# Hybrid decoder layer on one core: row sums for four more block and pair combinations, made by one task, and all pairs of two more FFN blocks in seven products

## The chip, the core and the metric

The kernel runs on one core of a Trainium2 chip. The metric is the device time of one execution in microseconds (us). The kernel before took 1103.51 us in the median of three runs (1102.64 to 1104.92). TensorE (PE in the profile) multiplies into PSUM banks, VectorE (DVE) and ScalarE (ACT) work element by element, GpSimd (POOL) does small steps and issues some transfers, SyncE (SP) issues most of the others. Each engine takes its own instructions in the order in which they were written for it.

## What is computed

One layer over 256 tokens of width 2048: an RMS norm and one input projection; gated linear attention (GLA) over four heads; native sparse attention (NSA) over eight heads, with compressed, selected and window branches; an output projection with a residual; and a SwiGLU feed-forward part (FFN) of width 5632. Cut to what the change touches:

```python
def compress(u, pos, w1, w2):                   # u: keys or values of two heads
    blocks = u[:, :, cmp_idx] + pos             # 15 overlapping blocks of 32 positions
    flat = blocks.reshape(b_, hk, n_cmp, CMP_BLOCK * dh)
    return jax.nn.silu(flat @ w1) @ w2
...
h = x + jnp.concatenate([gla_out, nsa_out], axis=-1) @ w_out
m = rms_norm(h, ffn_norm_g)
return h + (jax.nn.silu(m @ w_gate) * (m @ w_up)) @ w_down
```

## The kernel before

**Two parts for every number.** A float32 factor is split into a high and a low part of the type that TensorE takes at full rate. A product is then three matmuls: high by high, high by low, low by high. For a weight, ACT copies the high part and DVE subtracts it from the raw tile to get the low part: `hi` and `lo` at L144 and L145 before the FFN, `ftwo` at L654 and L655 in it. There are four `lo` buffers of two row tiles each, so DVE can be at most four ahead of PE.

**Stages.** Until about 290 us eleven projections with W_in are made (`proj`, its matmuls at L292 in `chunk`), from 290 to 413 us W_out in two halves of eight chunks (`w_out_half`), after that eleven FFN blocks of 512 columns. In FFN block f, `gate_up(f)` (matmuls at L1164) makes the products with W_gate and W_up; `down(f-1)` then makes those with W_down for the block before (L292 again).

**Seven products.** In `gate_up` the 2048 rows of the weights are taken as eight pairs of row tiles. A pair with two halves of the tokens, and W_gate and W_up, is a product of 2x2 tiles. A plain pair takes eight tile products, 24 matmuls. A pair in the table `FIRST7` takes seven (the scheme of Strassen and Winograd), 21 matmuls; it needs sums of the tokens (`pair_forms`, made once) and sums of the weights. Before, blocks 2 to 9 take pair 6 plainly and the other seven pairs in seven products, and block 10 takes all eight in seven. Their orders are ORDER1 = (0,1,2,6,3,4,5,7) and ORDER = (0,...,7); the constant `ALL7` is the first block that has all eight.

**Row sums.** The sums of the weights are made in one of two ways. Either DVE makes them in the FFN when the pair is due: L1195 (1024 columns), L1196 and L1197 (512 each). Or they were made ahead: a task `sum_rows(f, pair)` loads the four row tiles of W_gate and W_up with two transfers of 512 KB on SP (L1091), adds them in place with four DVE instructions (L1096), and stores two results of 512 KB to DRAM from POOL (L1100); in the FFN they are fetched by POOL one pair ahead (L1153). Such a pair then loads three row tiles rather than four. The table `SUMS` lists 16 of them: (0,4), (1,2) to (1,5), pair 7 of blocks 2 to 10, and pairs 2 and 5 of block 10.

**What sets the order.** `drive` runs a main task (a projection, a half of W_out, a block) and gives it side tasks: GLA, NSA and the compression come up after so many units of matmul work (2 units each), and the first of the list `background`, the row sums, after every `rate[0]` units. A `sum_rows` task needs nine calls: three between the loads and the first addition, one for each addition, one after the stores, and one that ends it. A scheduler below puts each engine's instructions in order by its own estimate of when they can run; so the orders shift a little around any edit.

**Compression.** `positions` (L780) adds the positions to 16 of 32 rows of a block for both heads, as a tile of 16 x 2 x 15. `compress` runs in two passes (keys, values) of two halves. In each half 32 matmuls at L796 (16 in the program, two in the trace for each, since float32 passes in two) load 30 columns of weights into one of four column groups of 32; DVE clears the bank ahead, at L788, since columns 30 and 31 of a group are never written but are read with the rest. The rows of the compression's weights come by POOL transfers (L771).

Of the kernel before, what the change touches and what calls it, by code (L numbers as in the profile page):

```python
# [8 lines left out]
F32 = mybir.dt.float32  # L9
# [3 lines left out]
ALU = mybir.AluOpType  # L13
AX = mybir.AxisListType

P = 128
# [10 lines left out]
NCMP = 15  # L27
# [10 lines left out]
def kernel(  # L38
# [736 lines left out]
    def positions(w, half, new):  # L775

        blk, j0 = new([16, 2, NCMP]), 16 * half
        for h in range(2):
            u = st["uT"][:, w, h, j0:j0 + 240].rearrange("p (n j) -> p j n", j=16)
            TT(blk[:, :, h, :], u, pos[:, w, j0:j0 + 16].unsqueeze(2).to_broadcast([P, 16, NCMP]), ALU.add)  # L780
        return blk

    def compress():

        nxt = [st["rows"], w1_rows(1)]
        for w in range(2):
            ph = bank()
            nc.vector.memset(ph[:, :P], 0.0)  # L788
            for half in range(2):
# [4 lines left out]
                for j in range(16):  # L794
                    g = 32 * (j % 4)
                    mm(ph[g:g + N2, :P], blk[:, j].rearrange("p h n -> p (h n)"), r[j // 8][:, j % 8, :], start=(half == 0 and j < 4),  # L796
                       stop=(half == 1 and j >= 12), tile_position=(0, g), skip_group_check=True)
                    if j % 16 == 15:
                        yield
# [217 lines left out]
    ALL7 = 10  # L1017
# [67 lines left out]
    def sum_rows(f, pair):  # L1085

        n_tiles[0] += 1
        gate, up = g4([2, 512]), g4([2, 512])
        for to, m in ((gate, w_gate), (up, w_up)):
            with behind(last["dma"]):  # L1090
                nc.sync.dma_start(to, m[0][2 * pair * P:(2 * pair + 2) * P, f * FB:(f + 1) * FB].rearrange("(k p) w -> p k w", p=P))  # L1091
        for _ in range(3):
            yield True
        for o, i in ((up[:, 0], up[:, 1]), (up[:, 1], gate[:, 1]), (gate[:, 1], up[:, 0]), (gate[:, 0], gate[:, 1])):
            with behind(last["d"]):
                TT(o, o, i, ALU.add)  # L1096
            yield True
        to = row_sums[f, pair] = [dp.tile([P, 2, 512], F32, name=f"sums{i}_{f}_{pair}") for i in range(2)]
        for part, a in zip(to, (up, gate)):
            nc.gpsimd.dma_start(part, a)  # L1100
        for _ in range(1):
            yield True
# [265 lines left out]
    background += [sum_rows(f, pair) for f in sorted(SUMS) for pair in SUMS[f]]  # L1368
    rate[0] = 12
# [3 lines left out]
    rate[0] = 26  # L1373
# [3 lines left out]
    rate[0] = 18  # L1377
# [5 lines left out]
    rate[0] = 14  # L1383
# [43 lines left out]
```

## Time and profile before

| what | us |
|---|---|
| median of three runs | 1103.51 |
| lowest, highest | 1102.64, 1104.92 |
| the profiled execution | 1103.67 |
| its span, first to last instruction | 1102.0 |
| PE busy, DVE busy, ACT busy, POOL busy | 1094.4, 991.5, 742.0, 73.1 |
| W_out's second half ends, FFN begins | 413 |
| an FFN block's period (blocks 8 and 9) | 61.95, 61.94 |

The profiled execution took 1.67 us more than its span, which lies before the first and after the last instruction. A row of a timeline gives the start, the duration, the engine, the line of the kernel, the operation and the tiles (output, arrow, inputs); in brackets stands how long the engine sat idle before it and what ended that. "SPq" or "PEq" is an engine's sequencer, which issues and waits. A row of stretches gives for each engine its busy time and the number of its instructions, then the granted clock, the share of the transfer engines and GB/s. Matmuls overlap: a matmul of 512 columns shows some 390 ns, but the next one starts 0.23 us after it, so PE's work is counted by starts. The granted clock is 1.00 throughout.

### The profile page before, as it was taken

The page shows a single profiled execution, that of the slowest core. Times are in us where ns is not written, and L with a number is a line of the kernel's source. Part 1 is how long each engine was busy: PE and PEld are TensorE (multiplying, and loading weights), DVE is VectorE, ACT ScalarE, POOL GpSimd, SP SyncE. Part 2 cuts the span into 40 slices and gives each one's busy share as a digit, 9 for nine tenths or more (in the row PEclk, how much of TensorE's full clock was granted, in tenths as well). Part 3 has the DMA queues.
Part 4 walks back from the last instruction along what each step waited for, and adds up shares of the span by engine and source line. Part 5 has one row for each costly group of instructions (what it writes and reads, how often), then busy time and mean ns, then how long its engine had stood idle before and what let it go on. Part 6 is the DMA issues. An engine that isn't in the chain of part 4 may idle for free.

```text
span 1102.0 us, 14594 instructions
## 1 busy us (share of the span) xinstructions
PE 1094.4 (99%) x5290; PEld 900.6 (82%) x5290; DVE 991.5 (90%) x1277; ACT 742.0 (67%) x1009; POOL 73.1 (7%) x134
## 2 busy tenths in 40 slices
PE   9999999999999999999999999999999999999998
PEld 8888888987787877888888888888888888888886
DVE  6678879987799688997999999999999999999997
ACT  6645557555675587667586866768586866768685
POOL 4110001132100000000000000000000000000000
PEclk9999999999999999999999999999999999999999
DMA  7999988467864547785566657576566657576773
GB/s 269 340 340 368 354 295 292 160 226 285 287 229 173 191 153 244 234 318 188 182 230 210 214 200 251 175 257 210 202 230 210 215 199 251 174 259 231 234 230 114
DMA packets 124850, 259.61 MB, mean 236 GB/s; under 512 B 6709, under 2 KB 8793, under 8 KB 124778
## 3 DMA queue, kind: packets, MB, share of 16 engines
q1 hardware_dynamic: 113514, 219.86, 58.3%
q0 software_dynamic: 10368, 37.75, 9.3%
q10 hardware_dynamic: 896, 1.07, 0.3%
q8 instruction: 41, 0.67, 0.2%
q14 instruction: 31, 0.25, 0.1%
HBM read 239.78 MB, written 18.87 MB: 235 GB/s over the span
## 4 chain that ended last, share of the span: by engine, by line
PE 94%; DVE 3%; DMA 1%; POOL 1%; ACT 1%; issue 1%; ACTq 0%; SPq 0%; DVEq 0%; POOLq 0%
PE bank L292 47%; PE bank L1164 39%; PE bank L217 3%; PE bank L1305 2%; PE bank L889 1%; PE bank L962 1%; POOL sm L220 1%; DMA raw<-in_w_in_dram 1%; DMA g<-in_w_up_dram 1%; DVE lo L145 0%; PE bank L597 0%; DVE g L637 0%; PE bank L796 0%; DVE g L592 0%; DVE g L638 0%
## 5 line engine op out<-in xcount | busy, mean ns | idle before, releaser
L1164 PE MATMUL bank<-ftwo,g 128*128 128x512 f32 x1848 | 431.7, 392 | 0.2 <-ACT ftwo L654 0.2
L1164 PEld LDWEIGHTS bank<-ftwo,g 128*128 128x128 f32 x1848 | 342.5, 188 | 76.5 <-DVE ftwo L655 3.3
L292 PE MATMUL bank<-hi,g 128*128 128x512 f32 (+1 forms) x1088 | 325.2, 377 | 0.5 <-ACT hi L332 0.5
L655 DVE TENSOR_TENSOR ftwo<-fraw,ftwo 128x1536 fp32r<-128x1536 f32 (+1 forms) x130 | 257.6, 1982 | 8.2 <-ACT ftwo L654 6.8
L654 ACT ACTIVATE ftwo<-fraw 128x1536 fp32r<-128x1536 f32 (+1 forms) x130 | 217.0, 1671 | 32.0 <-DMA fraw<-in_w_up_dram 22.9
L292 PE MATMUL bank<-ftwo,g 128*128 128x512 f32 x960 | 221.1, 391 | 0.0
L292 PEld LDWEIGHTS bank<-hi,g 128*128 128x128 f32 x1088 | 192.0, 188 | 31.1 <-issue 1.4
L292 PEld LDWEIGHTS bank<-ftwo,g 128*128 128x128 f32 x960 | 179.2, 188 | 39.2 <-ACT bank L1276 1.9
L292 PE MATMUL bank<-lo,g 128*128 128x512 f32 (+3 forms) x544 | 193.9, 376 | 0.4 <-DVE lo L333 0.3
L144 ACT ACTIVATE hi<-raw 128x1024 fp32r<-128x1024 f32 (+3 forms) x124 | 130.5, 1057 | 86.0 <-PE bank L292 64.1
L145 DVE TENSOR_TENSOR lo<-raw,hi 128x1024 fp32r<-128x1024 f32 (+3 forms) x124 | 149.7, 1217 | 35.3 <-ACT hi L144 34.8
L654 ACT ACTIVATE ftwo<-g 128x1024 fp32r<-128x1024 f32 x74 | 78.2, 1057 | 69.9 <-DVE g L1195 40.6
L292 PEld LDWEIGHTS bank<-lo,g 128*128 128x128 f32 x544 | 98.5, 189 | 15.0 <-DVE lo L333 0.8
L655 DVE TENSOR_TENSOR ftwo<-g,ftwo 128x1024 fp32r<-128x1024 f32 x74 | 90.2, 1218 | 10.5 <-ACT ftwo L654 10.5
L655 DVE TENSOR_TENSOR ftwo<-fsum,ftwo 128x1024 fp32r<-128x1024 f32 x74 | 90.1, 1217 | 0.0
L654 ACT ACTIVATE ftwo<-fsum 128x1024 fp32r<-128x1024 f32 x74 | 77.5, 1048 | 6.9 <-DVE fsum L1197 5.7
L1288 ACT COPY g<-bank 128x512 f32<-128x512 f32 x80 | 45.9, 589 | 38.8 <-PE bank L292 37.1
L1195 DVE TENSOR_TENSOR g<-fraw 128x1024 f32<-128x1024 f32 x56 | 67.4, 1216 | 0.0
L1276 ACT COPY bank<-g 128x512 f32<-128x512 f32 x80 | 45.2, 593 | 14.4 <-DVE f L1225 13.2
L654 ACT ACTIVATE g<-bank 128x512 fp32r<-128x512 f32 x46 | 27.2, 598 | 32.1 <-PE bank L217 26.6
L217 PE MATMUL bank<-ident,g 128*128 128x128 f32 (+3 forms) x230 | 43.3, 276 | 0.2 <-DVE g L737 0.2
L1153 POOL DMA_DIRECT2D g<-sums x16 | 8.5, 533 | 510.8 <-DVE ftwo L655 482.2
(244 smaller groups left out, 899.8 us busy)
## 6 DMA issues: line engine op xcount, KB each, us to landing
fraw<-in_w_gate_dram SPq DMA_DIRECT2D x86, 512.0 KB, 4.0
fraw<-in_w_down_dram SPq DMA_DIRECT2D x42, 1024.0 KB, 5.1
raw<-in_w_in_dram SPq DMA_DIRECT2D x36, 1024.0 KB, 7.6
fraw<-in_w_up_dram SPq DMA_DIRECT2D x70, 512.0 KB, 4.8
sums<-g POOLq DMA_DIRECT2D x32, 512.0 KB, 6.4
raw<-in_w_out_dram SPq DMA_DIRECT2D x16, 1024.0 KB, 5.2
g<-in_w_gate_dram SPq DMA_DIRECT2D x16, 512.0 KB, 7.3
g<-in_w_up_dram SPq DMA_DIRECT2D x16, 512.0 KB, 8.9
```

Source lines behind the costliest of these rows:

```text
L144: act(h[:, i:i + n], r[:, k + i:k + i + n], AF.Copy)
L145: last["d"] = TT(o[:, i:i + n], r[:, k + i:k + i + n], f32(h[:, i:i + n]), ALU.subtract)
L217: return nc.tensor.transpose(o, i, ident[:n, :n])
L220: nc.gpsimd.tensor_tensor(o, i, mhalf[:i.shape[0], :i.shape[1]], ALU.pow)
L292: last["mm"] = mm(bk[t], a[:, k, t * P:(t + 1) * P], m[:, off:off + w], start=(first_ and k == 0 and i == 0), stop=(end and k == 3 and i = ...
L654: act(hi, ps, AF.Copy)
L655: last["d"] = TT(lo, ps, f32(hi), ALU.subtract)
L1164: mm(banks[q], x, m, start=todo[q] == total[q], stop=todo[q] == 1)
L1195: TT(s1, r[:, 1:3], r[:, 3:4].to_broadcast([P, 2, 512]), ALU.add)
L1276: nc.scalar.copy(banks[qs[n][t]], h_sb[n][:, t, :])
L1288: nc.scalar.copy(h_sb[n][:, t, :], bs[t])
L1305: mm(bk, u, m, start=(first and i == 0), stop=(end and i == 2), skip_group_check=onto)
```

## The change

**FFN.** `ALL7` goes from 10 to 8. Blocks 8 and 9 then take all eight pairs in seven products, in ORDER, and `SUMS` gains (8,2), (8,5), (9,2), (9,5): 20 combinations.

**Row sums as one task.** `rows_for` issues the two loads; `all_sums` goes through the list, asks for the next combination's rows before it adds the present one's, and stores without a call of its own. Each combination now takes five calls, and the rates are 22, 46 and 32 units where they were 12, 26 and 18; the last stays 14, and is no longer set a second time.

**Compression.** The tile of `positions` is 16 x 32; POOL clears its last two columns, the matmuls load 32 columns, and the bank isn't cleared by DVE.

```diff
     def positions(w, half, new):
-        blk, j0 = new([16, 2, NCMP]), 16 * half
+        full, j0 = new([16, 32]), 16 * half
+        nc.gpsimd.memset(full[:, :, N2:], 0.0)
+        blk = full[:, :, :N2].rearrange("p j (h n) -> p j h n", h=2)
...
-        return blk
+        return full
     def compress():
...
-            nc.vector.memset(ph[:, :P], 0.0)
...
-                    mm(ph[g:g + N2, :P], blk[:, j].rearrange("p h n -> p (h n)"), r[j // 8][:, j % 8, :], start=(half == 0 and j < 4),
+                    mm(ph[g:g + 32, :P], blk[:, j], r[j // 8][:, j % 8, :], start=(half == 0 and j < 4),
...
-    ALL7 = 10
+    ALL7 = 8
...
-    def sum_rows(f, pair):
-        n_tiles[0] += 1
-        gate, up = g4([2, 512]), g4([2, 512])
-        for to, m in ((gate, w_gate), (up, w_up)):
+    def rows_for(f, pair):
+        res = g4([2, 512]), g4([2, 512])
+        for to, m in zip(res, (w_gate, w_up)):
             with behind(last["dma"]):
                 nc.sync.dma_start(to, m[0][2 * pair * P:(2 * pair + 2) * P, f * FB:(f + 1) * FB].rearrange("(k p) w -> p k w", p=P))
+        return res
+
+    def all_sums(todo):
+        nxt = rows_for(*todo[0])
         for _ in range(3):
             yield True
-        for o, i in (...):
-            with behind(last["d"]):
-                TT(o, o, i, ALU.add)
+        for at, (f, pair) in enumerate(todo):
+            gate, up = nxt
+            if at + 1 < len(todo):
+                nxt = rows_for(*todo[at + 1])
             yield True
-        to = row_sums[f, pair] = [...]
-        for part, a in zip(to, (up, gate)):
-            nc.gpsimd.dma_start(part, a)
-        for _ in range(1):
-            yield True
+            for o, i in (...):
+                with behind(last["d"]):
+                    TT(o, o, i, ALU.add)
+                yield True
+            to = row_sums[f, pair] = [...]
+            for part, a in zip(to, (up, gate)):
+                nc.gpsimd.dma_start(part, a)
...
-    background += [sum_rows(f, pair) for f in sorted(SUMS) for pair in SUMS[f]]
-    rate[0] = 12
+    background.append(all_sums([(f, pair) for f in sorted(SUMS) for pair in SUMS[f]]))
+    rate[0] = 22
...
-    rate[0] = 26
+    rate[0] = 46
...
-    rate[0] = 18
+    rate[0] = 32
```

The additions stand at L1106 in the changed program (L1096 before), the stores at L1110 (L1100), the fetches at L1161 (L1153); other lines of the later part move by 1 (to L1001) or by 8.

Three places show how the order moves. The first is DVE in W_out's first half, at its fourth chunk, whose first low part is `lo_3378` before and `lo_3385` after; `g_578` or `g_528` are rows being added, `sm` is NSA's soft-max, L655 makes low parts for NSA. Before:

```order
L915 TENSOR_TENSOR g_569_3239<-sm_3227,sm_3234 128x4x3x15
L921 TENSOR_SCALAR g_546_3123<-g_546_3123,sm_3242 128x256 x4
L921 TENSOR_SCALAR g_547_3124<-g_547_3124,sm_3242 128x256 x4
L655 TENSOR_TENSOR g_584_3286<-bank_3284,g_583_3285 128x512
L895 TENSOR_REDUCE sm_3330<-bank_3334 128x2
L145 TENSOR_TENSOR lo_3378<-raw_3375,hi_3377 128x2x512
L655 TENSOR_TENSOR g_572_3254<-bank_3255,g_571_3253 128x4x128
L896 TENSOR_SCALAR sm_3331<-sm_3330,sc_3022 128x2
L1096 TENSOR_TENSOR g_578_3266<-g_578_3266 128x512
```

And after:

```order
L922 TENSOR_SCALAR g_535_3127<-g_535_3127,sm_3243 128x256 x4
L655 TENSOR_TENSOR g_569_3284<-bank_3282,g_568_3283 128x512
L1106 TENSOR_TENSOR g_528_3088<-g_528_3088 128x512
L896 TENSOR_REDUCE sm_3337<-bank_3341 128x2
L896 TENSOR_REDUCE sm_3337<-bank_3357 128x2
L655 TENSOR_TENSOR g_560_3255<-bank_3256,g_559_3254 128x4x128
L1106 TENSOR_TENSOR g_528_3088<-g_528_3088,g_527_3087 128x512
L897 TENSOR_SCALAR sm_3338<-sm_3337,sc_3018 128x2 x2
L1106 TENSOR_TENSOR g_527_3087<-g_527_3087,g_528_3088 128x512
L145 TENSOR_TENSOR lo_3385<-raw_3382,hi_3384 128x2x512
```

Three additions and three NSA steps now stand ahead of this low part; two more additions do so further up, between it and the low part before it.

The second place is PE at the same chunk: L292 is W_out, L889 to L892 (L890 to L893 after) are NSA's scores, L217 transposes. Before:

```order
L892 MATMUL bank_3333<-kcm,g_561_3192 128x15
L292 MATMUL bank_3291<-hi_3377,g_438_2608 128x512
L292 MATMUL bank_3291<-lo_3378,g_438_2608 128x512
L889 MATMUL bank_3391<-g_318_1976,g_562_3193 128x256
L292 MATMUL bank_3291<-hi_3377,g_439_2609 128x512
```

And after:

```order
L893 MATMUL bank_3340<-kcm,g_549_3192 128x15
L292 MATMUL bank_3289<-hi_3384,g_426_2601 128x512
L890 MATMUL bank_3398<-g_307_1970,g_550_3193 128x256
L890 MATMUL bank_3398<-g_308_1971,g_550_3193 128x256
L292 MATMUL bank_3290<-hi_3384,g_426_2601 128x512
L890 MATMUL bank_3398<-g_307_1970,g_551_3194 128x256
L892 LDWEIGHTS identb
L892 MATMUL bank_3398<-cneg,identb 128x256
L893 MATMUL bank_3340<-kcm,g_549_3192 128x15
L217 MATMUL bank_3440<-ident,g_557_3240 79x128 x4
L217 MATMUL bank_3451<-ident,g_534_3126 128x128 x2
L217 MATMUL bank_3451<-ident,g_535_3127 128x128 x2
```

The next row after is the first use of `lo_3385`: five score matmuls, one of W_out and eight transposes were put ahead of it.

The third place is POOL around the compression: L220 raises to the power -1/2, L771 asks for rows of the compression's weights. Before:

```order
L220 TENSOR_TENSOR sm_2451<-sm_2451,mhalf 128x2
L771 DMA g_429_2539<-in_cmp_k_w_dram 128x8x128
L220 TENSOR_TENSOR sm_2480<-sm_2480,mhalf 128x2
L771 DMA g_430_2541<-in_cmp_k_w_dram 128x8x128
L771 DMA g_435_2599<-in_cmp_v_w_dram 128x8x128
L220 TENSOR_TENSOR sm_2530<-sm_2530,mhalf 128x2
L771 DMA g_436_2601<-in_cmp_v_w_dram 128x8x128
L1100 DMA sums_8_7_2639<-g_361_2231 128x1024
```

And after:

```order
L220 TENSOR_TENSOR sm_2475<-sm_2475,mhalf 128x2
L771 DMA g_417_2533<-in_cmp_k_w_dram 128x8x128
L220 TENSOR_TENSOR sm_2524<-sm_2524,mhalf 128x2
L771 DMA g_418_2535<-in_cmp_k_w_dram 128x8x128
L771 DMA g_423_2591<-in_cmp_v_w_dram 128x8x128
L771 DMA g_424_2593<-in_cmp_v_w_dram 128x8x128
L778 MEMSET g_425_2595 128x16x2
L778 MEMSET g_476_2817 128x16x2
L778 MEMSET g_482_2875 128x16x2
```

The second transfer of the keys' rows moves behind a third L220, and the clearing of the position tiles stands behind four transfers.

More of the change, by code (lines that the diff above doesn't have):

```diff
@@ L1083 @@
     row_sums = {}
-    def sum_rows(f, pair):
-        n_tiles[0] += 1
-        gate, up = g4([2, 512]), g4([2, 512])
-        for to, m in ((gate, w_gate), (up, w_up)):
+    def rows_for(f, pair):
+        res = g4([2, 512]), g4([2, 512])
+        for to, m in zip(res, (w_gate, w_up)):
             with behind(last["dma"]):
                 nc.sync.dma_start(to, m[0][2 * pair * P:(2 * pair + 2) * P, f * FB:(f + 1) * FB].rearrange("(k p) w -> p k w", p=P))
+        return res
+    def all_sums(todo):
+        nxt = rows_for(*todo[0])
         for _ in range(3):
             yield True
-        for o, i in ((up[:, 0], up[:, 1]), (up[:, 1], gate[:, 1]), (gate[:, 1], up[:, 0]), (gate[:, 0], gate[:, 1])):
-            with behind(last["d"]):
-                TT(o, o, i, ALU.add)
+        for at, (f, pair) in enumerate(todo):
+            gate, up = nxt
+            if at + 1 < len(todo):
+                nxt = rows_for(*todo[at + 1])
             yield True
-        to = row_sums[f, pair] = [dp.tile([P, 2, 512], F32, name=f"sums{i}_{f}_{pair}") for i in range(2)]
-        for part, a in zip(to, (up, gate)):
-            nc.gpsimd.dma_start(part, a)
-        for _ in range(1):
-            yield True
+            for o, i in ((up[:, 0], up[:, 1]), (up[:, 1], gate[:, 1]), (gate[:, 1], up[:, 0]), (gate[:, 0], gate[:, 1])):
+                with behind(last["d"]):
+                    TT(o, o, i, ALU.add)
+                yield True
+            to = row_sums[f, pair] = [dp.tile([P, 2, 512], F32, name=f"sums{i}_{f}_{pair}") for i in range(2)]
+            for part, a in zip(to, (up, gate)):
+                nc.gpsimd.dma_start(part, a)
     rf = kp.tile([P, NT], F32, name="rf")
@@ L1382 @@
     drain(later)
-    rate[0] = 14
     drive([w_out_half(1)], 6)
```

## The prediction

> **What bounds the kernel now.** I read the page first, then the chain in order of time, then what PE waited for.
>
> ```profile
> span 1102.0 us, 14594 instructions
> PE 1094.4 (99%) x5290; PEld 900.6 (82%) x5290; DVE 991.5 (90%) x1277; ACT 742.0 (67%) x1009; POOL 73.1 (7%) x134
> ...
> PE 94%; DVE 3%; DMA 1%; POOL 1%; ACT 1%; issue 1%; ACTq 0%; SPq 0%; DVEq 0%; POOLq 0%
> ```
>
> PE is busy for 99% of the span and holds 94% of the chain that ended last. A busy PE may still be a stalled one, so the list of its waits matters: it has six rows, and its two longest are
>
> ```profile
> PE bank L207 <- DVE g L201: 1.3, 1, 1.3
> PE bank L796 <- DVE g L780: 1.1, 1, 1.1
> ...
> ```
>
> The first is the start of the program. The second is the only wait in the change's reach that an earlier operand would shorten: one half of the compression. So the kernel lasts as long as its matmuls: what saves matmuls saves their full time, and what merely relieves another engine saves nearly nothing. The chain through the last FFN blocks shows what one saved product is worth. In block 9 and then in block 10 it reads:
>
> ```profile
> 956.88 0.22 PE bank L217 x2
> ...
> 960.54 32.88 PE bank L1164 x144
> ...
> 1022.45 32.22 PE bank L1164 x141
> ```
>
> Block 9 still has a plain pair and block 10 none: 144 against 141 matmuls in the long piece, all else equal. 32.88 us over 144 is 0.228 us a matmul, and 32.88 - 32.22 = 0.66 us is what the plain pair costs more.
>
> **FFN blocks 8 and 9.** Each loses one plain pair's 24 matmuls and gains 21, so 6 matmuls go: 6 x 0.228 = 1.37 us. The Trainium skill, page TensorE: Matmul & The Clock Gate, section Back-to-back issue gap, gives 131 ns as the sustained spacing of matmuls of 512 columns and 216 ns as the isolated one; by these the six would be an estimated 0.79 or 1.30 us, and the spacing of this trace decides against both. The term stands only if no other engine becomes late. Here are `gate_up` of blocks 9 and 10, then the whole periods:
>
> ```profile
> 953.36:993.42 40.06, 40.06 (x180) 32.64 (x180) 39.10 (x37) 27.65 (x26) 2.12 (x4) 1.00 0.64 221
> 1015.30:1054.67 39.37, 39.37 (x177) 31.99 (x177) 38.88 (x36) 29.17 (x28) 2.11 (x4) 1.00 0.71 228
> 953.36:1015.30 61.94, 61.94 (x276) 50.58 (x276) 60.62 (x57) 44.22 (x47) 2.12 (x4) 1.00 0.67 230
> 1015.30:1076.50 61.20, 61.20 (x277) 49.83 (x277) 58.77 (x62) 47.70 (x53) 2.11 (x4) 1.00 0.68 219
> ```
>
> DVE (the third pair of numbers) works 60.62 of block 9's 61.94 us. That is the resource to count. The forms of its instructions:
>
> ```profile
> L655 DVE TENSOR_TENSOR ftwo<-fraw,ftwo 128x1536 fp32r<-128x1536 f32 x74 | 129.8, 1754 | 3.6 <-ACT ftwo L654 2.9
> L655 DVE TENSOR_TENSOR ftwo<-fraw,ftwo 128x2048 fp32r<-128x2048 f32 x56 | 127.8, 2283 | 4.7 <-ACT ftwo L654 3.9
> L655 DVE TENSOR_TENSOR ftwo<-g,ftwo 128x1024 fp32r<-128x1024 f32 x74 | 90.2, 1218 | 10.5 <-ACT ftwo L654 10.5
> L655 DVE TENSOR_TENSOR ftwo<-fsum,ftwo 128x1024 fp32r<-128x1024 f32 x74 | 90.1, 1217 | 0.0
> L1195 DVE TENSOR_TENSOR g<-fraw 128x1024 f32<-128x1024 f32 x56 | 67.4, 1216 | 0.0
> L1197 DVE TENSOR_TENSOR fsum<-fsum,fraw 128x512 f32<-128x512 f32 x56 | 38.4, 686 | 0.9
> L1196 DVE TENSOR_TENSOR fsum<-g,fraw 128x512 f32<-128x512 f32 x56 | 38.3, 686 | 0.7
> ...
> L1240 DVE TENSOR_TENSOR f<-bank,f 128x512 f32<-128x512 f32 x21 | 14.3, 679 | 0.1
> ```
>
> Pair 6 gives up one of 2283 ns and takes one of 1754 and two of 1218 and 1217: +1.91 us, and sums of 1216 + 686 + 686 = 2.59 us. Pairs 2 and 5 lose these sums, -5.18 us, since theirs now come from DRAM. The plain pair's eighth bank isn't added any more (L1240): -0.68 us. Together -1.36 us a block, so DVE would work 59.3 us of 61.3. ACT, 44.22 us busy, has 17.7 idle for its own exchange (one copy of 2048 columns for one of 1536 and two of 1024). POOL fetches four more results a block, as block 10 does. Block 10 is the test that before already holds: its `gate_up` takes 39.37 us with all of PE busy. I take the full 1.37 us; below 0 and above 1.5 are excluded by that row.
>
> **Additions asked for ahead.** DVE's waits for the rows of the sums are the edit's plain target:
>
> ```profile
> DVE g L1096 <- DMA g<-in_w_up_dram: 11.6, 5, 5.1
> ```
>
> 11.6 us in five waits can go. They are DVE's, though, and no wait of PE names the weights' low parts (L145) that stood behind them: the four buffers covered them. Gain taken: 0. Until the end of the fifth projection the four-step additions do not get denser: by the 57th low part DVE has made 39 of them before and 36 after, in the stretch where the transfers are full:
>
> ```profile
> 87.00:110.00 23.00, 23.00 (x107) 19.04 (x106) 20.03 (x30) 13.06 (x19) 2.13 (x4) 1.00 0.98 362
> ```
>
> Asking one combination ahead puts about 1 MB earlier into that stream, 3 us at 362 GB/s, ahead of some weights of W_in. The rows that it delays are asked for three chunks ahead, so I take 0 here too, and 1 us at worst.
>
> **Four more combinations.** The 16 further additions fall into W_out's two halves:
>
> ```profile
> 306.88:316.54 9.66, 9.66 (x55) 7.62 (x54) 9.05 (x29) 7.56 (x15) 0.00 (x0) 1.00 0.90 315
> 310.00:350.00 40.00, 40.00 (x212) 31.93 (x211) 37.38 (x101) 24.76 (x61) 1.67 (x3) 1.00 0.65 238
> 350.00:386.00 36.00, 36.00 (x173) 29.50 (x172) 25.80 (x35) 19.23 (x29) 1.78 (x3) 1.00 0.52 176
> ```
>
> From 350 us on DVE has 10 us to spare in 36, and the transfers are half idle, which covers three combinations of four additions and 2 MB each. From 310 to 350 DVE has 2.6 us left in 40, and the tightest point lies at its entry, the fourth chunk of W_out:
>
> ```profile
> 316.54 1.21 DVE L145 TENSOR_TENSOR lo<-raw,hi 128x1024 fp32r<-128x1024 f32 x1
> ...
> 326.77 0.68 DVE L1096 TENSOR_TENSOR g<-g 128x512 f32<-128x512 f32 x1
> 327.37 0.21 DVE L909 TENSOR_REDUCE sm<-sm 128x4 f32<-128x60 f32 x1
> ```
> ```profile
> 319.07 0.28 PE L889 MATMUL bank<-g,g 128*128 128x256 f32 x1
> 319.19 0.40 PE L292 MATMUL bank<-lo,g 128*128 128x512 f32 x1
> ...
> 320.36 0.39 PE L292 MATMUL bank<-lo,g 128*128 128x512 f32 x1
> ```
>
> The low part ends at 316.54 + 1.21 = 317.75, and PE first uses it at 320.36: 2.6 us of slack. In the new order five additions at 0.60 (326.77 to 327.37) and NSA steps of about 1.2 us (one L655, as long as an addition, and four short ones) stand ahead of it, 4.2 us, less the 0.6 us that DVE idles in 306.88 to 316.54: 3.6 us later, 1.0 us too late by itself. But PE's order moves with it: eight transposes (0.22 a pair, 0.88), a matmul (0.23) and five score matmuls (0.12 each from 319.07 to 319.19, 0.6) now come first, 1.7 us. So the low part should be in time by about 0.7 us. I take 0 for W_out, and 4.2 us as the other end, if nothing covers; a gain is excluded, as no wait of PE lies here.
>
> **Compression.** The wait of 1.1 us that PE has here comes from this order on DVE:
>
> ```profile
> 251.85 0.68 DVE L1096 TENSOR_TENSOR g<-g 128x512 f32<-128x512 f32 x1
> 252.45 1.01 DVE L780 TENSOR_TENSOR g<-g,cols 128x240 f32<-128x240 f32 x2
> 253.38 1.22 DVE L145 TENSOR_TENSOR lo<-raw,hi 128x1024 fp32r<-128x1024 f32 x1
> ```
> ```profile
> 253.52 1.08 PE L796 MATMUL bank<-g,g 128*30 128x128 f32 x32 [1.10 <-DVE g L780]
> ```
>
> In the changed order the addition stands behind L780, so the positions are ready 0.60 us earlier: -0.6 us. Against it stands POOL, where the second transfer of the keys' rows moves behind a third power step:
>
> ```profile
> 246.14 1.62 POOL L220 TENSOR_TENSOR sm<-sm,mhalf 128x2 f32<-128x2 f32 x1 [0.83 <-DVE sm L631]
> 247.72 0.92 POOL L771 DMA_DIRECT2D g<-in_cmp_v_w_dram  x1
> ```
> ```profile
> DMA to landing us min/median/max: 4.7/6.7/9.1
> ```
>
> The last row is for all eight transfers of these rows. Behind the power step this one is issued at 247.72 (where before asks for rows of the values) and lands 4.7 to 9.1 us later, at 252.4, 254.4 or 256.8. It holds the second half of the rows, which PE needed 0.5 us after 253.52, at 254.0. So the half ends 0.6 us earlier, 0.4 or 2.8 us later than before. I take the median, +0.4 us. The cleared tile is ready in time: four transfers of 0.92 us, less the first, and a short clear end at 250.7, and the bank's own clear was waited for by nobody.
>
> The matmuls load 32 columns for 30:
>
> ```profile
> L796 PEld LDWEIGHTS bank<-g,g x128: 104/108/108, 247.2 to 281.0; 128*30 128x30 f32 x128
> ```
>
> A load takes 108 ns, four at a time in four column groups. The Trainium skill, page TensorE: Matmul & The Clock Gate, section LDWEIGHTS (loading the stationary operand), has a load grow with its columns, P/1.2 ns; by that the change adds an estimated 1.7 ns a load, 0.2 us over 128. The row is four times what that formula gives for 30 columns (25 ns), so I go by the row. Four groups of matmuls of 1.08 us each, longer by 2 columns in 30, give 4 x 1.08 x 2/30 = 0.3 us if the loads set the pace and 0 if they don't; I take 0.1.
>
> **The sum.** -1.37 (FFN) + 0.4 (compression) + 0.1 (columns) = -0.87 us. From the profiled execution's 1103.67 that is 1102.8; its median stands 0.16 lower, at 1103.51, so the forecast is **1102.7 us**. About 0.2%, 2.2 us, is what a measurement of this kernel can tell from no change, since its three runs lie 2.3 us apart; the forecast is inside it.
>
> **Rivals.**
>
> *DVE falls behind in W_out (slower).* If NSA's steps can't run early enough for PE's new order, since the score matmuls and transposes put ahead wait for DVE themselves, nothing covers the additions at the fourth chunk, and PE waits the 4.2 us: 1103.67 - 1.37 + 0.5 + 4.2 = 1107.0. For it speaks DVE's 37.38 of 40 us; against it that no wait of PE lies here now and that the transposes read what the soft-max steps had finished by then. It turns the gain into a loss once PE waits more than 0.9 us there. 0.10.
>
> *The compression's rows land late.* The second transfer takes 9.1 us like the slowest: 1103.67 - 1.37 + 2.8 + 0.1 = 1105.2. Against it: that row is from all eight, and the slowest of them may lie where the transfers were full. 0.08.
>
> *They land early.* Then only the positions decide, and the wait shrinks by 0.6: 1103.67 - 1.37 - 0.6 = 1101.7. For it speaks 4.7 us, the fastest; the transfer needs 5.7 us or less. 0.30.
>
> *The sums aren't there.* A combination that isn't stored when its block is written would be summed on DVE: pairs 2 and 5 then cost 5.18 us again, and a block would need 60.62 - 1.36 + 5.18 = 64.4 us of DVE against 61.3 of PE, 3.1 us twice: 1103.67 + 2 x 3.1 - 0.87 + 1.37 = 1110.4. POOL's order has all twenty pairs of stores ahead of the first fetch, so 0.01.
>
> **How the numbers follow.** The forecast keeps 0.51. A median of three scatters by some 0.7 us here. Under 1101.3 (faster by over 0.2%) lie a third of the early case, 0.10, and 0.03 of the forecast's; over 1105.7 lie 0.08 of W_out's case and 0.02 of the late case. That is 0.13 faster, 0.10 slower and 0.77 the same. The range goes from 1101.0, the early case less the scatter, to 1105.0, just short of the late case; what it leaves out above is W_out's case and half of the late one.
>
> **What would show it.** In the changed profile, the long piece of L1164 in blocks 8 and 9 counts 141 matmuls and 32.2 us, and the periods are 61.3; if they are 61.9, DVE or a fetch is late and the FFN term falls. DVE's wait for rows of the sums is gone or below 2 us, with PE's time before the FFN the same. PE's row at the compression's second half shows a wait between 0.5 and 1.5 us, by a transfer rather than by L780. W_out shows no wait of PE over 0.5 us near 320 us. The forecast is wrong if the first FFN matmul of the long series comes more than 2 us earlier or later than now while the blocks behave.

## The result: 0.8% slower

The changed kernel took 1112.66 us in the median of five runs (1111.27 to 1113.06), the kernel before 1102.75 (1102.52 to 1104.92) beside it: a ratio of 1.0082, 95% interval 1.007 to 1.0093. The forecast was 1102.7 us, in a range of 1101.0 to 1105.0. The profiled execution of the changed kernel took 1111.27 us, its span is 1109.5.

The profile after, first the page:

```profile
span 1109.5 us, 14659 instructions
...
PE 1094.3 (99%) x5284; PEld 898.9 (81%) x5284; DVE 997.9 (90%) x1287; ACT 743.4 (67%) x1013; POOL 81.7 (7%) x154
...
PE 87%; DVE 5%; DMA 4%; issue 2%; ACT 1%; POOL 1%; SPq 0%; ACTq 0%; DVEq 0%; POOLq 0%
```

PE's busy time is the same to 0.1 us. Its share of the chain that ended last fell from 94 to 87%: DVE (3 to 5%) and DMA (1 to 4%) hold more of it. The FFN isn't where that comes from. The chain through blocks 8 and 9 (start, duration, what, how many):

```profile
900.32 3.54 PE bank L1172 x15
...
907.51 32.32 PE bank L1172 x141
...
961.62 3.54 PE bank L1172 x15
...
968.82 32.28 PE bank L1172 x141
```

141 matmuls in 32.3 us, and the period of block 8 is 961.62 - 900.32 = 61.30 us: as forecast. To find the loss I took three low parts (`lo`) and read on PE's timeline when the same one is first used. Before:

```profile
185.85 0.39 PE L292 MATMUL bank<-lo,g 128*128 128x512 f32 x1
...
255.45 0.48 PE L292 MATMUL bank<-lo,g 128*128 128x512 f32 x1
...
410.64 0.39 PE L292 MATMUL bank<-lo,g 128*128 128x512 f32 x1
```

And after:

```profile
185.51 0.39 PE L292 MATMUL bank<-lo,g 128*128 128x512 f32 x1
...
261.66 0.48 PE L292 MATMUL bank<-lo,g 128*128 128x512 f32 x1
...
418.94 0.39 PE L292 MATMUL bank<-lo,g 128*128 128x512 f32 x1
```

The lag, after less before, is -0.34, 6.21 and 8.30 us. So 6.55 us are lost between 186 and 255 us, in the stretch where GLA and NSA's keys run beside the projections, and 2.09 from there to the end of W_out; the granted clock is 1.00 in both. The first FFN blocks add 0.7 (block 2's first product comes 107.09 us after block 0's, 106.40 before), blocks 8 and 9 take 1.3 off, and the program up to 186 us gave 0.3; that is 7.7 us, close to the 7.5 by which the span grew. What the engines wait for, the rows that are new:

```profile
ACT g L748 <- DMA sums<-g: 6.3, 1, 6.3
POOL g L771 <- DMA sums<-g: 5.9, 1, 5.9
...
DVE g L855 <- DMA sums<-g: 3.5, 1, 3.5
...
PE bank L597 <- ACT g L610: 3.4, 1, 3.4
...
ACT g L873 <- DMA sums<-g: 3.0, 1, 3.0
...
DVE g L713 <- DMA sums<-g: 2.4, 1, 2.4
```

`sums<-g` is the store of a finished sum to DRAM. L748 and L713 write tiles of NSA's keys and values, L855 and L873 its queries, L771 the compression's rows. None of them reads anything of the sums; what links them is the buffer. All these tiles and the rows of the sums come from the one pool of 24 slots of 4 KB, `g4`, and a slot can be written again only when the store out of it has landed. Before, no engine waits for a store. Of these waits only those at L713 and L748 end between 186 and 255 us. POOL's at L771 ended at 172.87 us, those at L855 and L873 at 274.6 and 283.9, and PE's lag doesn't move at any of the three: a wait in this list costs something only where PE stands behind it. It does behind L713, whose store was issued at 198.47 and took 5.40 us. DVE, then PE:

```profile
203.96 0.48 DVE L713 SCALAR_TENSOR_TENSOR g<-bank,rx,g 128x256 fp32r<-128x256 f32 x1 [2.45 <-DMA sums<-g]
```
```profile
211.99 0.50 PE L217 MATMUL bank<-ident,g 128*128 128x128 f32 x2 [1.47 <-DVE g L737]
```

DVE's steps of NSA's keys (L737) come later behind L713, and PE's transposes, which waited 0.16 us for them before, wait 1.47; the lag goes from -0.34 to 1.61 us. The timelines of POOL, ACT and PE show the dearest of the waits:

```profile
223.04 0.58 POOL L1110 DMA_DIRECT2D sums<-g  x1 [12.04 <-DVE g L1106]
```
```profile
230.60 0.84 ACT L748 ACTIVATE g<-bank,kgain 128x256 fp32r<-128x256 f32 x2 [6.27 <-DMA sums<-g]
...
232.28 0.28 ACT L610 ACTIVATE g<-bank 128x128 f32<-128x128 f32 x1
```
```profile
232.60 0.71 PE L597 MATMUL bank<-g,g 128*128 128x128 f32 x4 [3.40 <-ACT g L610]
```

ACT reached the key's tile at 224.3, the store had been issued 1.3 us before and landed at 230.5. ACT's next copy for GLA (L610) stood behind it in the queue, and PE's GLA matmuls behind that; the lag is 1.47 us before this and 6.13 behind it. In the kernel before the same line ran at 212.51 without a wait:

```profile
212.51 0.82 ACT L748 ACTIVATE g<-bank,kgain 128x256 fp32r<-128x256 f32 x2
```

### The profile page after: what moved, and what is told of

It reads as the page before. It is cut to its first block, busy times and chain, and to the rows that moved or that the text cites. A ratio compares the mean times of both kernels' runs of the same rounds, so it can differ in the third digit from the quotient of the medians.

```text
span 1109.5 us, 14659 instructions
## 1 busy us (share of the span) xinstructions
PE 1094.3 (99%) x5284; PEld 898.9 (81%) x5284; DVE 997.9 (90%) x1287; ACT 743.4 (67%) x1013; POOL 81.7 (7%) x154
## 2 busy tenths in 40 slices
DMA packets 128818, 271.15 MB, mean 244 GB/s; under 512 B 7093, under 2 KB 9177, under 8 KB 128746
## 4 chain that ended last, share of the span: by engine, by line
PE 87%; DVE 5%; DMA 4%; issue 2%; ACT 1%; POOL 1%; SPq 0%; ACTq 0%; DVEq 0%; POOLq 0%
PE bank L292 41%; PE bank L1172 39%; PE bank L217 3%; PE bank L1313 2%; DVE lo L145 2%; DMA sums<-g 1%; DMA raw<-in_w_out_dram 1%; DMA g<-in_w_up_dram 1%; PE bank L890 1%; DVE g L1106 1%; POOL sm L220 1%; DMA g<-in_cmp_k_w_dram 1%; DMA raw<-in_w_in_dram 0%; PE bank L963 0%; ACT hi L144 0%
## 5 line engine op out<-in xcount | busy, mean ns | idle before, releaser
L292 PE MATMUL bank<-hi,g 128*128 128x512 f32 (+1 forms) x1088 | 321.0, 375 | 0.8 <-ACT hi L332 0.8
L655 DVE TENSOR_TENSOR ftwo<-fraw,ftwo 128x1536 fp32r<-128x1536 f32 (+1 forms) x130 | 256.5, 1974 | 8.0 <-ACT ftwo L654 7.0
L292 PE MATMUL bank<-ftwo,g 128*128 128x512 f32 x960 | 220.9, 390 | 0.0
L292 PEld LDWEIGHTS bank<-hi,g 128*128 128x128 f32 x1088 | 191.9, 188 | 31.0 <-ACT hi L332 1.2
L292 PEld LDWEIGHTS bank<-ftwo,g 128*128 128x128 f32 x960 | 179.4, 188 | 38.8 <-ACT bank L1284 1.5
L292 PE MATMUL bank<-lo,g 128*128 128x512 f32 (+3 forms) x544 | 193.7, 375 | 0.3 <-DVE lo L145 0.2
L292 PEld LDWEIGHTS bank<-lo,g 128*128 128x128 f32 x544 | 98.3, 188 | 15.0 <-DVE lo L145 0.9
L655 DVE TENSOR_TENSOR ftwo<-g,ftwo 128x1024 fp32r<-128x1024 f32 x76 | 92.6, 1219 | 10.7 <-ACT ftwo L654 10.7
L655 DVE TENSOR_TENSOR ftwo<-fsum,ftwo 128x1024 fp32r<-128x1024 f32 x76 | 92.5, 1217 | 1.2 <-ACT ftwo L654 1.2
L1203 DVE TENSOR_TENSOR g<-fraw 128x1024 f32<-128x1024 f32 x54 | 65.1, 1217 | 0.2 <-DMA fraw<-in_w_up_dram 0.2
L1161 POOL DMA_DIRECT2D g<-sums x20 | 10.6, 530 | 502.2 <-DVE ftwo L655 473.6
L217 PE MATMUL bank<-ident,g 128*128 128x128 f32 (+3 forms) x230 | 42.3, 277 | 3.1 <-ACT g L1061 1.5
```

The source lines that it names most:

```text
L217: return nc.tensor.transpose(o, i, ident[:n, :n])
L292: last["mm"] = mm(bk[t], a[:, k, t * P:(t + 1) * P], m[:, off:off + w], start=(first_ and k == 0 and i == 0), stop=(end and k == 3 and i = ...
L655: last["d"] = TT(lo, ps, f32(hi), ALU.subtract)
L1203: TT(s1, r[:, 1:3], r[:, 3:4].to_broadcast([P, 2, 512]), ALU.add)
```

## The experiments

The theory after this reading: asking ahead keeps four slots in the hands of the sums where two were, so that other tiles get slots which a store has only just left, and in-order queues behind them pass that wait on to PE. The rivals: four more combinations in the same stretch; the compression; and the spacing or the phase of the additions. In the table "ratio" is against the kernel before on the same chip; "waits" is the sum of the rows "<- DMA sums<-g"; the two lags are those gained from the low part at 186 us to that at 255, and from there to that at 411; "first FFN" is the time from block 0's first product to block 2's (106.40 before).

| kernel | asks ahead at the keys | ratio, 95% interval | waits | 186-255 | 255-411 | first FFN |
|---|---|---|---|---|---|---|
| the change | yes | 1.0082, 1.007 to 1.0093 | 21.1 | 6.55 | 2.09 | 107.09 |
| ahead_16 | yes | 1.0082, 1.0063 to 1.01 | 18.8 | 6.48 | 0.87 | 106.43 |
| after_old_cmp | yes | 1.0087, 1.0072 to 1.0102 | 21.0 | 8.33 | 1.94 | 107.06 |
| w_out_26 | yes | 1.0086, 1.0071 to 1.0101 | 19.0 | 5.67 | -0.48 | 112.53 |
| phase_40 | yes | 1.0045, 1.003 to 1.006 | 3.7 | 5.14 | 1.15 | 106.45 |
| phase_52 | yes | 1.0044, 1.003 to 1.0058 | 7.4 | 3.61 | 2.15 | 106.48 |
| ahead_8 | yes | 1.0041, 1.0026 to 1.0057 | 8.9 | 3.90 | 1.39 | 106.70 |
| own_slot | yes | 1.0078, 1.0062 to 1.0095 | 8.4 | 3.53 | 3.93 | 109.37 |
| fewer_small_slots | yes | 1.019, 1.0174 to 1.0207 | 18.7 | 17.07 | 6.13 | 107.05 |
| no_ahead | no | 1.0033, 1.0016 to 1.0049 | 0 | -0.32 | 0.22 | 106.49 |
| hold_slots | no | 1.0046, 1.0032 to 1.0059 | 0 | -0.59 | 0.09 | 106.50 |
| spaced | no | 1.0004, 0.9995 to 1.0013 | 0 | 0.34 | 1.11 | 106.38 |
| ahead_early | no | 1.0014, 1.0005 to 1.0023 | 2.2 | 0.20 | 0.04 | 108.30 |
| early_dense | no | 1.0008, 0.9999 to 1.0017 | 2.0 | 0.68 | 0.23 | 107.49 |
| split | no | 1.0019, 1.001 to 1.0027 | 0 | 0.90 | 1.62 | 106.45 |
| split_old_cmp | no | 1.0013, 1.0004 to 1.0022 | 0 | 0.58 | 2.34 | 106.44 |
| old_20 | no | 0.9994, 0.9984 to 1.0003 | 0 | -0.53 | -0.30 | 107.17 |
| old_20_cmp | no | 1.0002, 0.9993 to 1.0011 | 0 | 0.38 | -0.31 | 107.13 |
| old_20_dense | no | 1.0011, 1.0003 to 1.002 | 0 | -0.43 | 1.42 | 107.65 |

Read down the fourth and fifth columns: the nine kernels that ask ahead there all wait for stores and lose 3.5 to 17 us in that stretch; the ten that don't (two of them with a single wait of 2 us) lose at most 0.9.

That stretch ends behind the compression, which moves by itself from run to run. Up to a low part just before it (251.35 us before the change) eight of the nine lose 4.1 to 19.8 us (the change 6.20, own_slot 5.89), and phase_52 only 1.46. Of the ten, the three whose additions stand 46 units apart (spaced, split, split_old_cmp) lose 1.4 to 2.0 there, the others at most 0.7. So by this measure phase_52 can't be told from the kernels that don't ask ahead.

**Taking the change apart.** *no_ahead*: one task, 20 combinations, the rows asked for when the turn comes.

```diff
-            gate, up = nxt
-            if at + 1 < len(todo):
-                nxt = rows_for(*todo[at + 1])
-            yield True
+            gate, up = rows_for(f, pair)
+            for _ in range(4):
+                yield True
```

The rates go from 22, 46, 32, 14 to 14, 29, 20, 9.

> The changed kernel, but the rows of a combination are asked for when its turn comes: eight calls a combination with rates 14, 29, 20 and 9, so that the twenty combinations come as often as in the changed kernel. Theory (asking ahead): each combination in flight holds four of the 24 slots of the g4 pool rather than two, and a tile that takes over such a slot must wait until the store out of it has landed; the three waits for stores between 198 and 260 us go, the first FFN matmul comes near 427 us, and the time is 1102 to 1104 us. Rival 1 (four more combinations in the same stretch load DVE and the transfers): all twenty are still there, so 1109 to 1112. Rival 2 (compression): unchanged, 1112. Rival 3 (chance of where the stores fall beside the other tiles): anything between 1102 and 1112, with waits for stores elsewhere.

1107.84 us, outside the 1102 to 1104 of the theory; the ten runs lie anywhere from 1103.70 to 1111.05. The stretch from 186 us is clean, but 5.7 us are lost earlier, by the very wait that the change was to remove. DVE and PE:

```profile
135.57 0.69 DVE L1102 TENSOR_TENSOR g<-g 128x512 f32<-128x512 f32 x1 [4.46 <-DMA g<-in_w_up_dram]
```
```profile
142.24 1.11 PE L217 MATMUL bank<-ident,g 128*128 128x128 f32 x4 [4.16 <-ACT g L520]
```

The convolution's steps (L501) stood behind that addition on DVE, ACT's L520 behind them, PE's transposes behind that. So this run alone doesn't decide; ahead_8, below, repeats it with one difference.

*ahead_16*: `ALL7 = 10`. *old_20*: the kernel before with `ALL7 = 8`. *after_old_cmp*: the changed kernel with the three edits of the compression undone.

> The changed kernel with ALL7 back at 10: 16 combinations, rows still asked for ahead. Theory (asking ahead): the wait of ACT for a store near 224 us, 6.3 us, is there as before the edit, the FFN begins some 7 to 9 us late, and the time is the changed kernel's plus the 1.4 us of the two FFN blocks, less up to 2 us in W_out: 1111 to 1114 us. Rival 1 (four more combinations): 1103 to 1105. Rival 2 (compression): 1113.

> The kernel before with ALL7 = 8 alone: 20 combinations by the old tasks at the old rates, no asking ahead, old compression. Theory (asking ahead): the FFN's 1.37 us are gained and nothing is lost, 1101 to 1102 us. Rival 1 (four more combinations): they lie in W_out's second half and in the FFN's beginning here, so a loss of 1 to 3 us, 1103 to 1105. Rival 2 (compression): 1101.4.

> The changed kernel with the compression as it was before. Theory (asking ahead): the losses before 250 us and in W_out stay, 1111 to 1113 us. Rival 2 (compression): 1102 to 1104.

1112.51, 1102.74 and 1113.57 us; old_20 lies between the range of the theory and that of its rival, after_old_cmp 0.6 us above its range. The first stretch loses the same with 16 combinations, and nothing with 20 by the old tasks; the compression's edit isn't the cause. Four more combinations are the cause of something smaller: between ahead_16 and the change, 1.2 us in W_out and 0.7 in the first FFN blocks, 1.9 us, against 1.3 that the blocks 8 and 9 save. So the two kernels can't be told apart in their times.

**Is it the slot?** *own_slot* gives the keys' high parts a slot outside the pool; its 4 KB come from other pools, and *fewer_small_slots* is the control with these smaller pools alone.

```diff
-... slot(s2p, "g2", 13), slot(s1p, "g1", 7), ...
+... slot(s2p, "g2", 12), slot(s1p, "g1", 5), ...
+    own = slot(s2p, "own", 1, LINE)
...
-                    st[name] = g4(shape, F32R)
+                    st[name] = (own if name == "kh" else g4)(shape, F32R)
```

> The changed kernel, but the tile of the high parts of the keys (kh, which ACT writes at L748 and for which it waited 6.3 us for a store) has a slot of its own instead of one of the 24; its 4 KB come from one fewer g2 slot and two fewer g1 slots. Theory (the slot's hand-over): ACT's wait at that line goes, PE's wait at L597 of 3.4 us with it, the lag that PE shows against the kernel before stays near 1.5 us after 223 us instead of jumping to 6.1, and the time is 1107 to 1109 us. Rival (DVE and the transfers are late there by their load alone): another wait takes its place, the lag jumps all the same, 1111 to 1113 us.

> The control for the kernel with the slot of its own: the changed kernel with 12 g2 and 5 g1 slots (13 and 7), and the keys' tile in the g4 pool as in the change. Both theories: 1111 to 1114 us, ACT's wait for a store near 224 us still there. If it is below 1110, the smaller pools and not the slot moved the time.

1112.72 and 1124.78 us. own_slot's time lies where the rival had it, and its lag at 233 us is 6.05 us, not the 1.5 of the theory (6.12 in the change): ACT's wait is gone, as the theory had it, and the time isn't. The control, which missed its range by 11 us, shows why this can't be read against the change: with the smaller pools both kernels are already late before the keys' tiles come, 4.04 us and 4.48 at 222 us where the change is 1.47. From there to 233 us own_slot loses 2.0 us and the control 15.3. In their source the two differ in the one slot alone (the scheduler also moves some of their instructions), and in total by 12 us. In the control the keys' low parts (L750 there, L749 in the change) wait for a store, and PE behind them. The waits of the control:

```profile
PE bank L598 <- DVE g L750: 10.8, 1, 10.8
...
DVE g L750 <- DMA sums<-g: 6.8, 1, 6.8
```

In own_slot these two rows are 0.8 and 0.7. It doesn't return to the time of the kernel before, as the other tiles still take slots from the pool. A kernel with 25 slots and the other pools as they were wasn't run.

*phase_40* and *phase_52* change the middle rate from 46 to 40 and 52 units, so that the sums run sooner or later against the other tasks.

> The changed kernel with the middle rate at 40 units rather than 46: asking ahead and 20 combinations as in the change, but from the second drive on the sums run some 13% sooner against the other tasks, so that another tile takes the slot that a store has just left. If asking ahead costs by holding slots whatever the place, the lag at 230 us is 4 to 7 us again and the time 1110 to 1113. If it is a matter of which tile meets which store, the jump at 223 us goes or moves, and the time lies between 1103 and 1109 us or another wait for a store is in the list.

> The changed kernel with the middle rate at 52 units rather than 46: the sums run some 13% later against the other tasks, asking ahead as in the change. In this order ACT's first write of the keys' high parts takes a slot that no store has left. If the place decides which tile meets which store, the jump at 223 us goes and 4 to 6 us with it, 1106 to 1109 us, the rest being W_out's density. If asking ahead costs by itself, 1111 to 1113.

1108.95 and 1108.02 us. The wait of ACT is gone in both. In phase_40 another tile has it instead; on DVE's timeline and on PE's:

```profile
229.54 0.88 DVE L749 SCALAR_TENSOR_TENSOR g<-bank,kgain,g 128x256 fp32r<-128x256 f32 x2 [3.66 <-DMA sums<-g]
```
```profile
230.17 0.68 PE L597 MATMUL bank<-g,g 128*128 128x128 f32 x4 [2.37 <-DVE g L749]
```

In phase_52 the only wait for a store in the stretch is DVE's at L713, 0.81 us. POOL's longer one ended at 178.98 us, and PE's lag doesn't move on it. Of the 3.61 us, 1.46 are lost before the compression and 2.15 at it, where PE waits for a transfer that POOL issued late, behind DVE and not behind a store. POOL, then PE:

```profile
178.98 0.90 POOL L771 DMA_DIRECT2D g<-in_cmp_k_w_dram  x1 [6.62 <-DMA sums<-g]
...
252.73 0.94 POOL L771 DMA_DIRECT2D g<-in_cmp_k_w_dram  x1 [1.90 <-DVE g L638]
```
```profile
257.28 0.65 PE L797 MATMUL bank<-g,g 128*32 128x128 f32 x16 [1.20 <-DMA g<-in_cmp_k_w_dram]
```

The phase decides who waits for a store and for how much: at most 6.27 us, 3.66 or 0.81. The whole loss in the stretch is above 3.6 us at all three, but at 52 units most of it doesn't come from a store.

**Asking ahead or spacing?** With five calls the additions stand further apart as well (46 units, where eight calls have 29). *hold_slots* was to hold four slots without early transfers; the two programs' instructions turn out to have one order and the same waits on every engine, so it is a second measurement of no_ahead and tells nothing of held slots.

> As the kernel that asks when the turn comes (rates 14, 29, 20, 9), but the two slots of the next combination are taken one combination ahead and stay empty until its turn: four slots are held as in the change, and no transfer runs early. If held slots alone delay other tiles, waits for stores appear again between 198 and 260 us and the time is 1110 to 1115. If it takes the store that comes late just where a tile wants its slot, there is no such wait here, and the time is that of the kernel without asking ahead, 1106 to 1109.

1108.19 us, against 1107.84. *ahead_8* is no_ahead with the rows asked for one combination earlier; *spaced* asks ahead up to the fifth long projection and has five calls, 46 units apart, without it from there.

```diff
             if at + 1 < len(todo):
                 nxt = rows_for(*todo[at + 1])
-            yield True
+            for _ in range(4):
+                yield True
```

> The changed kernel's asking ahead, with eight calls a combination at rates 14, 29, 20 and 9: it differs from no_ahead in nothing but that the rows are asked for one combination earlier. If asking ahead makes the loss at 223 us, a wait for a store is back between 198 and 260 us with a lag of 4 to 6 us, and, as the rows are there at 139 us, the time is that of no_ahead, 1107 to 1110. If the spacing of the additions makes it, no such wait, no loss at 139 us either, and W_out's 0.5 to 1 us alone is left: 1102 to 1104.

> Asks ahead up to the fifth of the long projections, and from there asks when the turn comes, but with five calls at the change's rates 46, 32 and 14, so that the additions stand 46 units apart. If the spacing makes the loss, a wait for a store of 3 us or more appears between 198 and 260 us and the lag at 233 us is 4 to 7 us: 1107 to 1111. If asking ahead makes it, the lag there stays below 2 us, and W_out's density (70 units a combination) costs its 0.5 to 2.5: 1103 to 1106.

1108.01 and 1104.29 us. ahead_8 against no_ahead is the cleanest pair of the study: from 131 to 186 us the lag grows by 0.20 instead of 5.66, from 186 to 255 by 3.90 instead of -0.32 (up to the compression by 4.10 instead of -0.87), and the medians agree to 0.2 us, though no_ahead's runs scatter by 7 us and ahead_8's by 0.2. Asking ahead buys one wait and pays with another. DVE's timeline in ahead_8:

```profile
205.07 0.48 DVE L713 SCALAR_TENSOR_TENSOR g<-bank,rx,g 128x256 fp32r<-128x256 f32 x1 [3.35 <-DMA sums<-g]
```

spaced shows that wide spacing alone doesn't make the loss: it loses 1.43 us up to the compression, where the change loses 6.20, and gets 1.10 back at it, as PE comes later and no longer waits there. It is 8 us faster than the change.

**W_out and the four combinations.** In the change a combination comes every 70 units in W_out, 126 before. The stretch from 350 to 386 us, of which the prediction said that the transfers are half idle:

```profile
350.00:386.00 36.00, 36.00 (x175) 29.26 (x174) 34.38 (x62) 18.58 (x32) 3.80 (x7) 1.00 0.91 323
```

DVE works 34.38 us there instead of 25.80, the transfers are 91% busy instead of 52. A W_out row then takes 11.08 us to land (chain), beside three stores of sums issued at 377.94, 380.88 and 381.48 us; ACT waits for it, and PE for ACT:

```profile
378.81 11.08 DMA raw<-in_w_out_dram
```
```profile
390.00 1.06 ACT L144 ACTIVATE hi<-raw 128x1024 fp32r<-128x1024 f32 x1 [3.08 <-DMA raw<-in_w_out_dram]
390.96 1.32 ACT L1061 ACTIVATE g<-g,hscale 128x512 f32<-128x512 f32 x2
```
```profile
391.72 0.33 PE L217 MATMUL bank<-ident,g 128*128 128x128 f32 x1 [1.50 <-ACT g L1061]
```

*w_out_26* sets the last rate from 14 to 26.

> The changed kernel with the last rate at 26 units rather than 14: in W_out a combination comes every 130 units as before the change (9 calls of 14), not every 70. Theory (in W_out the loss of some 2.7 us is the density of the sums: rows, stores and additions next to the weights' own rows): the lag gained between 300 and 400 us falls to 1 us or less, 1110 to 1111 us in all. Rival (the lag there comes from the shifted order alone): 1112 to 1113.

1113.34 us. W_out's loss goes, as the theory had it (-0.48), and the total doesn't: seven of the forty stores now run after 390 us (none in the change), and the first FFN blocks take 6 us longer. POOL issues a store and then the fetch that stood behind it, and PE, behind ACT, waits 1.88 us for that fetch; where the rest of the 6 us comes from isn't traced here:

```profile
480.31 0.54 POOL L1110 DMA_DIRECT2D sums<-g  x1 [4.08 <-DVE f L1036]
480.83 1.57 POOL L1161 DMA_DIRECT2D g<-sums  x3
```
```profile
488.45 4.09 PE L1172 MATMUL bank<-ftwo,g 128*128 128x512 f32 x11 [1.88 <-ACT ftwo L654]
```

The other runs look for a place where the four combinations cost less than they save. *ahead_early*: as spaced, but eight calls (29, 20, 16). *old_20_cmp*: old_20 with the new compression. *early_dense*: ahead_early with 9 in W_out's second half. *old_20_dense*: old_20 with 8 there. *split*: spaced with 24 in the first half and 12 in the second. *split_old_cmp*: the same with the old compression.

> The changed kernel, but rows are asked for ahead only in the drive of the first five of the long projections (where the kernel before let DVE wait 11.6 us for them); from there on each combination asks when its turn comes and takes eight calls, at rates 29, 20 and 16, so that in W_out one comes every 128 units as before the change. Theory (two causes: slots held over the keys' tiles, and density in W_out): no jump at 223 us, no lag gained in W_out, FFN gain 1.4 us, compression 0.3 us better: 1101 to 1103 us. Rival (asking ahead itself is the cause wherever it is): a lag of 4 us or more before 180 us, 1106 or above.

> The kernel before with ALL7 = 8 and the new compression, old tasks and rates. Theory: the FFN's 1.4 us and the positions' 0.3 to 0.6 us are gained and nothing is lost: 1101 to 1102.7 us. Rival (a late second transfer of the keys' rows eats the positions' gain): 1102.5 to 1103.

> ahead_early with the rate of W_out's second half at 9 rather than 16: a combination comes every 72 units there, all twenty are stored before the FFN. Theory: W_out's second half covers them when nothing is asked ahead (no_ahead gained no lag there), and the first FFN blocks take 106.4 us again rather than 108.3: 1102.7 to 1103.7. Rival (the second half's density costs what it saves): 1104.5 to 1105.5.

> old_20 with the rate of W_out's second half at 8 rather than 14, so that the four more combinations are stored before the FFN. Theory: the first FFN blocks take 106.4 us rather than 107.2 and nothing is lost in W_out: 1101.5 to 1102.3, below the kernel before. Rival (a loss of 1 us or more in W_out's second half): 1102.7 to 1104.

> spaced (asks ahead up to the fifth long projection only) with the last rate at 24 units in W_out's first half and 12 in its second, so that a combination comes every 120 and then every 60 units. Theory (the first half is where they cost): lag gained between 255 and 410 us 0 to 0.5 us rather than 1.1, first FFN blocks 106.4 us, 1102.5 to 1103.7 us. Rival (the second half costs as much when it is as dense): 1104 to 1105.

> The same with the compression as before the change. If the new compression is worth the 0.3 us by which the prediction had the positions earlier less the transfer, 0.3 us above split; if the late second transfer of the keys' rows costs more than the positions gain, 0.3 to 1 us below split.

1105.15, 1103.44, 1104.64, 1104.84, 1105.32 and 1105.17 us. All six are within 0.2% of the kernel before, and none is faster; the five whose theory named a range of times came out 0.7 to 2.5 us above it. The four combinations cost 1.1 to 2.3 us in W_out where they are dense (spaced, split, split_old_cmp, old_20_dense), or 0.7 to 1.9 us of the first FFN blocks where they are left for it (old_20, ahead_early); early_dense loses 1.1 in the first FFN blocks and 0.2 in W_out. That is as much as the 1.3 us that they save. The nearest to a gain is old_20, 0.9994 (0.9984 to 1.0003), which beats the change by 0.9% and isn't to be told from the kernel before. The compression's edit can't be told from none either: split and split_old_cmp, or old_20_cmp and old_20, have overlapping intervals.

## Why the prediction was wrong

**The step that failed** is "Additions asked for ahead", where it says: "The rows that it delays are asked for three chunks ahead, so I take 0 here too, and 1 us at worst." It priced the early transfers and the DVE waits, and both prices held: the waits went from 11.6 to 0.4 us, and up to 186 us PE was not late. It did not price the slots. Two more tiles of a pool of 24 are held, each of them until a store has landed, and the prediction named neither the pool nor who else draws on it. In place of 0 the runs showed 6.55 us, nearly all of it behind two waits for a store (L713, then L748). That asking ahead does it is shown (ahead_8 against no_ahead, spaced against the change), and that a slot's hand-over can cost such a sum is too, in a kernel with smaller pools (own_slot against its control); that one tile's slot is the whole of it isn't so, as own_slot was as late as the change. That it is the number of held slots, rather than the moment of the hand-over that shifts with it, is argued from the waits and wasn't isolated. Full transfers aren't the reason: between the two low parts they were busy 58% of the time, 65% before. The Trainium skill, page Trainium Kernel Development and Optimization, section Best Practices, advises to double-buffer, so that transfers lie beside compute; the transfers did, and the second buffer came out of others' supply. The Trainium skill, page Perfetto Trace Analysis, section Optimization Strategy, takes a gap that repeats on the busy engine for a possible sign that there is no room for the next tile. Here PE's gaps in the stretch were 1.47, 0.25, 0.58 and 3.40 us up to the compression, at different lines and behind different engines, not one gap that repeats; the sign to go by was the releaser in the rows of DVE and ACT, a transfer of a tile that the waiting instruction doesn't use.

**"I take 0 for W_out"** was wrong by 2.1 us, and the first FFN blocks by 0.7, inside the 4.2 us kept as the other end, but mostly elsewhere. At the fourth chunk, where the prediction looked, the low part was 0.06 us ahead of its use (0.7 computed), and PE's lag, 8.35 us there, fell back to 6.64 at the next one. By 361 us the lag settles at 7.1 us, 0.9 above that before W_out; PE's rows show 0.18 us of idle time for it, and what made the rest isn't traced. The other 1.2 us came at 390 us, in the stretch whose "10 us to spare" the prediction read as cover: on average there was room, but a row of the weights shared the transfers with three stores of sums and landed late.

**The FFN term was right**: 61.30 and 61.28 us a block, 1.3 us for both, 1.37 forecast; DVE works 59.89 of 61.30 us, 59.3 forecast, and no wait came of it.

**The compression was right in mechanism, and near in size.** The second transfer of the keys' rows stands behind POOL's third power step, and PE waits for it rather than for the positions. POOL, then PE:

```profile
252.12 1.61 POOL L220 TENSOR_TENSOR sm<-sm,mhalf 128x2 f32<-128x2 f32 x1 [2.96 <-DVE sm L631]
253.70 0.94 POOL L771 DMA_DIRECT2D g<-in_cmp_k_w_dram  x1
```
```profile
260.15 0.64 PE L797 MATMUL bank<-g,g 128*32 128x128 f32 x16 [0.56 <-DMA g<-in_cmp_k_w_dram]
```

It landed 6.41 us after it was issued (6.7 taken), and the lag grew by 0.36 us from the low part before it to the one behind it; +0.5 was forecast with the 32 columns. In other orders the same step gave from -2.7 (fewer_small_slots) to +2.15 us (phase_52), so the size holds for this order alone.

**The rivals.** W_out's got the sign and the place in the program, but not the mechanism nor most of the sum. None of the rivals looked at the pool. The forecast itself is rounded up: 1103.51 - 0.87 is 1102.64 us, and the prediction wrote 1102.7.

## What to carry to other kernels

A prefetch has two prices: the transfer, and the buffer for as long as it is held, until the last reader, a store too, has landed. Before asking ahead, list who else draws on the same pool during that time and which in-order queues stand behind them. And a stretch that is half idle on average hides a transfer only if nothing with a due time runs beside it just then.

## What the runs showed of the hardware

The time from issue to landing isn't a constant to plan with: in the kernel before the rows of W_out took 5.2 us in the median and in the changed one 6.7, up to the 11.08 above, though the bytes moved grew only from 259.61 to 271.15 MB. Stores of 512 KB out of the slots took 5.40 to 7.49 us in the chain of the changed kernel, and the next user of a slot waits for the landing, not the issue: the store issued at 223.04 us landed at 230.53, and ACT's L748 began at 230.60.
